# Selection moved, attention's background doubled, and the last output columns done block by block, in a one-core transformer block

## The chip, the cores and the metric

The kernel runs on one core of one Trainium2 chip. The metric is the device time of one execution in microseconds (us), as the median of several runs; lower is better. The engines are TensorE (PE in the profile; PEld is its weight load), VectorE (DVE), ScalarE (ACT), GpSimd (POOL) and SyncE (SP), whose queue issues most of the DMAs.

## The reference

One block of a streaming encoder on `x` of 512 tokens x 4096, float32:

```
h = rmsnorm(x);  z = h @ w_in      # 4096 x 9808: q, c, qi, kix, wix, gate_a, pool_in, gate_b
I[t,s] = sum_h wix[t,h] * relu(qi[t,h] . kix[s])       # indexer, 16 heads of 64
sel    = the 128 best s of each t with s//64 <= t//64
ya[h]  = softmax(q[h] . (c[sel] w_uk[h])) @ c[sel] w_uv[h]      # 16 heads of 128, latent c of 512
yb     = ((trailing mean over 2/4/8/16 tokens - token) @ w_pool[g]) * scale     # 4 groups of 512
y      = [ya * silu(gate_a), yb * silu(gate_b)] @ w_out;  out = x + rmsnorm(y)
```

## The kernel before

All matmuls keep float32 accuracy: `split` (L67) makes of each operand a high part (a ScalarE cast to fp32r) and a low part (a VectorE subtraction), and `mm3` (L80) does three matmuls of them. Tiles of 128 x 512 are the unit; `ts(b, P)` is block b of 128.

The stages, with their times in the profile before:

- *First projection* (to about 130 us): latent `c` and the indexer's key. `staged` (L71) loads 256 KB of weights into the pool `st` and splits them; `st` lies on the right side of SBUF, which is filled downwards from the top of the memory (`side="right"`); `big` tiles with tags p0 to p7 and d0 to d7 lie on the left.
- *Indexer queries* (to 300) with `dots` on the background queue, and four gate groups (to 373).
- *Products* (373 to 976): the first 16 k-blocks of the remaining 60 groups are multiplied with seven products instead of eight (`PRODUCTS`, L337), in 120 steps of 42 matmuls of 256 columns (loop L475). `s_weights` loads the weights two steps ahead; `form_weights` (L340) makes three differences on VectorE (L341 to L343) and splits into `wh` and `wl`, 2 casts and 2 subtractions. `collect_z` (L459) sums the products; GpSimd's queue stores them in `zpd`. The operands are `xp` (p slots) and `xs` (d slots: slot di is read in the steps with t = i//2). In the last pair the k-blocks 16 to 31 come back from `xsp` into the p slots, eight loads of 1 MB on GpSimd's queue (L491).
- *Pooling mixer, groups 0 to 2* (993 to about 1280). `group` (L299) loads the stored part of a group into a `zt` slot, `stream` (L270) adds the other 16 k-blocks (48 matmuls of 512 columns) with weights from `st`, and steps the background queue `bg` (L314) at three places of four and once after the end.
- *Attention* (first score at 1278, last at 1828): the loop L744 does two groups for each of 16 heads (query, gate); `attn` (L693) of a head is a generator on `bg`: two steps of keys, four of scores and softmax, for each fourth head four of values, four of transposes (L733) and products, two at the end. `bg.drain()` finishes what the groups left.
- *Pool group 3* (to 1945) with `st3` on the left side, and sums for the next stage copied into d slots (`sums_early`).
- *Output, first 20 k-blocks* (to about 2354) as seven products over `order`.
- *Output, last 12 k-blocks* (EB; to 2630): for each of 8 column blocks db, all 12 k-blocks e times the row blocks b. W (`wout[db, e]`) is loaded and split by `prefetch` into a ring of four (`rot_raw`, `rot_hi`, `rot_lo`). `lanes` (L806) gives db 0 to 5 all four row blocks at once; db 6 and 7 come twice, first for blocks 0 and 1, then for 2 and 3. After a lane VectorE adds the first part, ScalarE sums the squares, and `yg` keeps the product with the post gain. `finish` (L902) forms the row norm, does `yg * ry + x` and stores; for blocks 0 and 1 it runs on `bg` during the last lanes, for 2 and 3 behind the last matmul.

`select` (L510) repeats 16 times: the eight largest scores of a row (MAX8) and their replacement, for three row blocks; then it writes the mask `mb`. It is traced behind the products and added to `bg`. The framework fixes the order of each engine's instructions when the program is built: in the order of the trace, but a ready instruction may be put into an engine's modelled gap ahead of earlier ones that aren't ready. A tile's slot is given to the next tile when all its readers are done.

Of the kernel before, what the change touches and what calls it, by code (L numbers as in the profile page):

```python
# [36 lines left out]
NFULL = 6  # L37
# [4 lines left out]
NFS = 4  # L42
# [10 lines left out]
def block_kernel(ctx: ExitStack, tc: tile.TileContext, xT, x, gk, wc, wkw, wf, ws, wd, wuk, wuv, kvn,  # L53
# [4 lines left out]
    bigp = ctx.enter_context(tc.tile_pool(name="big", bufs=1))  # L58
    st_stack = ctx.enter_context(ExitStack())
# [279 lines left out]

    def form_weights(w, pool, bufs=1):  # L340
        V.tensor_sub(w[:, 4:6], w[:, 1:3], w[:, 0:2])  # L341
        V.tensor_sub(w[:, 6], w[:, 2], w[:, 4])
        V.tensor_sub(w[:, 7], w[:, 3], w[:, 6])  # L343
        hi = pool.tile([P, 7, H], F32R, tag="wh", name="wh", bufs=bufs)
        lo = pool.tile([P, 7, H], F32R, tag="wl", name="wl", bufs=bufs)
        split(w[:, 0:3:2], hi[:, 0:2], lo[:, 0:2])
        split(w[:, 3:8], hi[:, 2:7], lo[:, 2:7])
        return hi, lo
# [124 lines left out]

    with tc.tile_pool(name="pa", bufs=2, side="right", reuse_waits="tile") as pa:
        for n, (m, t) in enumerate(order_s):  # L475
# [24 lines left out]
            if n + 2 < len(order_s):  # L500
                first[n + 2] = s_weights(n + 2)
            bg.step()
        bg.drain()
    wa_stack.close()
    st_stack = ctx.enter_context(ExitStack())
    st = st_stack.enter_context(tc.tile_pool(name="st", bufs=4, side="right", reuse_waits="tile"))
    zt["tags"] = ("d6", "d7")
    mb = big("d5", [P, OFF[4]], "mb", F32)

    def select():  # L510
        V.memset(mb[:, :P], 0.0)
        V.memset(mb[:CHUNK, CHUNK:P], NEG)
        for b in range(1, NB):
            V.memset(isc[:CHUNK, OFF[b + 1] - P - CHUNK:OFF[b + 1] - P], INADM)
        yield
        for r in range(TOPK // 8):
            for b in range(1, NB):
                o = score(b)
                m8 = kixp.tile([P, 8], F32, name="m8", bufs=4)
                V.max(m8, o)  # L520
                V.match_replace(o, m8, o, TAKEN)
                if b != 2:
                    yield
        for b in range(1, NB):
            V.tensor_scalar(mb[:, OFF[b]:OFF[b + 1]], score(b), -3.2e38, NEG,
                            op0=ALU.is_gt, op1=ALU.mult)
            yield

    bg.add(select())
# [10 lines left out]

    ops = {}
# [37 lines left out]
    def pool_group(pl, pm, g):  # L579
# [77 lines left out]
        def rest():  # L657
            def early(q):
                if q == 2:
                    for e in sum_part(7, ow, "wr", 2, lambda sh, n: big("d6", sh, n)):  # L660
                        pass

            zt.update(n=0, tags=("d7",))
# [26 lines left out]
    with tc.tile_pool(name="at", bufs=1, reuse_waits="tile") as at:  # L690
# [53 lines left out]
        for h in range(NH):  # L744
# [8 lines left out]
            group(Q + h, evac)  # L753
            sg = at.tile([P, S], F32, tag="sg", name="sga", bufs=2)
            bg.add(attn(h, qp, sg))
            group(GA + h, lambda z, sg=sg: gate(at, z, sg))
# [6 lines left out]
    with tc.tile_pool(name="pl1", bufs=1, reuse_waits="tile") as pl:  # L763
# [4 lines left out]
        def sums_early():  # L768
# [4 lines left out]
            for t in range(6):  # L773
                for w in sum_part(t + 1, cw, "cw", 1, lambda sh, n: big(f"d{t}", sh, n)):
                    yield
# [30 lines left out]
    lanes = [(db, (0, 1, 2, 3)) for db in range(NFULL)]  # L806
    lanes += [(db, p) for p in ((0, 1), (2, 3)) for db in range(NFULL, 8)]
    steps = [(n, e) for n in range(len(lanes)) for e in range(EB)]
# [11 lines left out]
    def rot_split(src, hi=None, lo=None):  # L820
        raw = rotate("raw", "p0", F32)
        nc.sync.dma_start(raw, src)
        if hi is None:
            hi, lo = rotate("hi", "d0", F32R), rotate("lo", "p1", F32R)
# [3 lines left out]
    CT = ("d1", "p2", "d2", "p3", "d3", "p4")  # L828
    SPARE = ("d4", "p5", "d5", "p6", "d6", "p7", "d7")
# [9 lines left out]
    def prefetch(n):  # L839
        if n < len(steps) and n not in ahead:  # L840
            lane, e = steps[n]
            if n < EB:
                load_cat(e)
            ahead[n] = rot_split(wout[lanes[lane][0], e])

    for n, (db, i) in enumerate(order):
# [11 lines left out]
        if db == 0:  # L858
            if i == 0:
                pure_part(7, load_quads(7, oc, "pt", 1), lambda sh, m: big("p6", sh, m))  # L860
            if i == 1:
                late = sum_part(8, oc, "pt", 1, lambda sh, m: big("d7", sh, m))
# [22 lines left out]
    home, yg, xs, pp = {}, {}, {}, {}  # L885
# [7 lines left out]
    def fetch():  # L893
        for m, (b, db) in enumerate([(b, db) for p in ((0, 1), (2, 3)) for db in range(8) for b in p]):
            if m < 16:
                xs[b, db] = spare(2 * NFULL + m)
            else:
                xs[b, db] = opl.tile([P, 512], F32, name=f"xr{m}")
            nc.sync.dma_start(xs[b, db], x[b, db])
            yield  # L900
# [16 lines left out]
    for n, (lane, e) in enumerate(steps):  # L917
        db, blocks = lanes[lane]
        if e == 0:
            yp = [bank("acc" if i == 3 else "w") for i in range(len(blocks))]  # L920
            if lane == 1:
                bg.add(fetch())
            if lane == NFULL + 8 - NFULL:
                bg.add(finish((0, 1)))
        prefetch(n)
        wo = ahead.pop(n)
        for i, b in enumerate(blocks):
            mm3(yp[i], tuple(t[:, ts(b, P)] for t in ct[e]), wo, e == 0, e == EB - 1)
        if e == 3:
            pg = opl.tile([P, 512], F32, name="pg", bufs=2)  # L930
            nc.sync.dma_start(pg, gpost[:, ts(db, 512)].to_broadcast([P, 512]))
            for b in blocks:
                pp[b] = opl.tile([P, 512], F32, name="pp", bufs=6)
                nc.sync.dma_start(pp[b].rearrange("p (a c) -> p a c", a=2),
                                  part[db, :, b // 2::2, ts(b % 2, H)])
        if e == EB - 1:
            prefetch(n + 1)
            prefetch(n + 2)
            for i, b in enumerate(blocks):
                V.tensor_add(pp[b], yp[i], pp[b])  # L940
            for i, b in enumerate(blocks):
                junk = opl.tile([P, 512], mybir.dt.bfloat16, name="junk")
                A.activation(junk, pp[b], AF.Square, accum_out=yss[b][:, db:db + 1])
# [85 lines left out]
```

## Time and profile before

| what | value |
|---|---|
| median of 3 runs | 2641.9 us (2641.01 to 2643.49) |
| profiled execution, own time | 2648.14 us |
| its span | 2646.4 us |
| TensorE busy | 2554.5 us, 97% |
| VectorE busy | 1718.2 us, 65% |
| ScalarE busy | 1046.7 us, 40% |
| granted TensorE clock, mean | 0.984 |
| DMA | 377.39 MB, 143 GB/s |

Shares are averages over the stages. Matmuls are pipelined: their printed duration is longer than the distance to the next, so their rate is read from the starts or from a count in a stretch. Some matmul records can be missing.

### The profile page before, as it was taken

Reading aid. Unit: us, or ns where it says so; the run is one execution under the profiler, and the core shown is the slowest. Engines: PE = TensorE matmul, PEld = TensorE weight load, DVE = VectorE, ACT = ScalarE, POOL = GpSimd, SP = SyncE. Lnnn points to the kernel's source line nnn. Section 1 sums busy time; section 2 is a strip of 40 time slices with the busy share of each in tenths; the row PEclk is TensorE's granted clock in tenths of the full one; section 3 lists DMA queues with packets and bytes.
Section 4 is the critical chain, followed back from the end, with each engine's and each line's share of the span. In section 5 each row is a group of like instructions: output and inputs, shape, how many; then the busy total and the mean of one; then the engine's idle time right before and its main releaser. Section 6 shows DMA issues by size and latency. Waiting matters only on the chain. (4 is left out here: it accounts for less than half of the span.)

```text
span 2646.4 us, 39505 instructions
## 1 busy us (share of the span) xinstructions
PE 2554.5 (97%) x15322; PEld 2267.3 (86%) x15322; DVE 1718.2 (65%) x3034; ACT 1046.7 (40%) x1724; POOL 77.6 (3%) x138
## 2 busy tenths in 40 slices
PE   9999999999999979999999999987999999999996
PEld 7799889999999977888888888765789999998875
DVE  5465798878888765554445454555787877864347
ACT  6444524444444433222333333333344444443333
POOL 0000001000000010000000000000000000000000
PEclk9999999999999999999999999988999999999998
DMA  9733423433433463444333333312453433386457
GB/s 329 261 114 110 155 80 130 134 128 131 141 128 130 135 256 126 143 129 121 117 103 105 99 100 101 99 60 76 159 160 120 136 121 120 134 268 198 139 161 245
DMA packets 167260, 377.39 MB, mean 143 GB/s; under 512 B 19872, under 2 KB 28192, under 8 KB 165024
## 3 DMA queue, kind: packets, MB, share of 16 engines
q1 hardware_dynamic: 156736, 332.92, 39.1%
q0 software_dynamic: 10336, 41.95, 4.3%
q8 instruction: 120, 1.97, 0.3%
q14 instruction: 68, 0.56, 0.1%
HBM read 324.46 MB, written 50.33 MB: 142 GB/s over the span
## 5 line engine op out<-in xcount | busy, mean ns | idle before, releaser
L68 ACT CAST wh<-wr 128x512 fp32r<-128x512 f32 (+1 forms) x400 | 362.1, 943 | 488.0 <-PE ps_acc L488 265.6
L69 DVE TENSOR_TENSOR lo<-raw,hi 128x512 fp32r<-128x512 f32 x416 | 286.1, 689 | 396.3 <-ACT hi L68 396.0
L69 DVE TENSOR_TENSOR wl<-wr,wh 128x512 fp32r<-128x512 f32 (+1 forms) x400 | 434.9, 1088 | 122.4 <-ACT wh L68 120.3
L68 ACT CAST hi<-raw 128x512 fp32r<-128x512 f32 x416 | 257.1, 619 | 614.5 <-PE ps_acc L83 417.9
L82 PE MATMUL ps_acc<-xr,hi 128*128 128x512 f32 x928 | 373.6, 403 | 21.5 <-ACT hi L68 21.5
L83 PE MATMUL ps_acc<-xr,hi 128*128 128x512 f32 x928 | 368.6, 397 | 0.0
L84 PE MATMUL ps_acc<-xr,lo 128*128 128x512 f32 x928 | 368.1, 397 | 0.0
L82 PEld LDWEIGHTS ps_acc<-xr,hi 128*128 128x128 f32 x928 | 176.5, 190 | 60.2 <-ACT hi L68 21.9
L84 PEld LDWEIGHTS ps_acc<-xr,lo 128*128 128x128 f32 x928 | 175.8, 189 | 42.6 <-DVE lo L69 0.5
L83 PEld LDWEIGHTS ps_acc<-xr,hi 128*128 128x128 f32 x928 | 176.2, 190 | 38.5
L487 PE MATMUL ps_w<-xp,wl 128*128 128x256 f32 x720 | 203.8, 283 | 5.4 <-DVE wl L69 5.3
L486 PE MATMUL ps_w<-xp,wh 128*128 128x256 f32 x720 | 203.2, 282 | 0.0
L488 PE MATMUL ps_w<-xp,wh 128*128 128x256 f32 x720 | 203.2, 282 | 0.0
L488 PE MATMUL ps_w<-xs,wh 128*128 128x256 f32 x720 | 203.1, 282 | 0.0
L487 PE MATMUL ps_w<-xs,wl 128*128 128x256 f32 x720 | 202.9, 282 | 0.0
L486 PE MATMUL ps_w<-xs,wh 128*128 128x256 f32 x720 | 202.8, 282 | 0.0
L341 DVE TENSOR_TENSOR wr<-wr 128x512 f32<-128x512 f32 x200 | 137.7, 689 | 54.1 <-DMA wr<-in_ws 27.7
L69 DVE TENSOR_TENSOR rot_lo<-rot_raw,rot_hi 128x512 fp32r<-128x512 f32 x120 | 80.8, 689 | 139.6 <-ACT rot_hi L68 139.4
L487 PEld LDWEIGHTS ps_w<-xp,wl 128*128 128x128 f32 x720 | 136.2, 189 | 6.4 <-DVE wl L69 6.4
L854 PE MATMUL ps_w<-wl,op 128*128 128x256 f32 x480 | 136.9, 285 | 4.2 <-DVE wl L69 4.1
L68 ACT CAST rot_hi<-rot_raw 128x512 fp32r<-128x512 f32 x120 | 74.1, 621 | 168.5 <-PE ps_acc L84 112.8
L486 PEld LDWEIGHTS ps_w<-xp,wh 128*128 128x128 f32 x720 | 136.1, 189 | 0.0
(310 smaller groups left out, 6002.4 us busy)
## 6 DMA issues: line engine op xcount, KB each, us to landing
wr<-in_ws SPq DMA_DIRECT2D x120, 512.0 KB, 3.4
raw<-in_wd SPq DMA_DIRECT2D x240, 256.0 KB, 2.6
wr<-in_wq SPq DMA_DIRECT2D x80, 512.0 KB, 3.5
rot_raw<-in_wout SPq DMA_DIRECT2D x120, 256.0 KB, 3.4
raw<-in_wf SPq DMA_DIRECT2D x96, 256.0 KB, 2.6
zt<-zpd SPq DMA_DIRECT2D x60, 256.0 KB, 2.7
cw<-cat SPq DMA_DIRECT2D x34, 256.0 KB, 3.0
raw<-in_wc SPq DMA_DIRECT2D x32, 256.0 KB, 5.6
```

What stands on the lines that cost most here:

```text
L68: A.copy(hi, src)
L69: V.tensor_sub(lo, src, hi.bitcast(F32))
L82: nc.tensor.matmul(dst, lh, rh, start=start, stop=False)
L83: nc.tensor.matmul(dst, lh, rl, start=False, stop=False)
L84: nc.tensor.matmul(dst, ll, rh, start=False, stop=stop)
L341: V.tensor_sub(w[:, 4:6], w[:, 1:3], w[:, 0:2])
L486: nc.tensor.matmul(zz, w0, x0, start=i == 0 and j % 2 == 0, stop=False)
L487: nc.tensor.matmul(zz, w1, x0, start=False, stop=False)
L488: nc.tensor.matmul(zz, w0, x1, start=False, stop=last)
L854: nc.tensor.matmul(zz, ab[0], wl[:, w], start=False, stop=False)
```

## The change

1. A tile `edge` of 8 floats per partition (32 bytes) is put at the top of the right side, so all other tiles there lie 32 bytes lower.
2. `select` runs in the loop of the products: its first part at step 6, its instructions placed behind the first difference of the last `form_weights` (`issue_after`); one further part at each third step. `mb` lies in d2 instead of d5, and is written at the end of it.
3. `zt` uses d0 and d1 instead of d6 and d7; the later uses of the d slots are permuted (`DT`).
4. In attention the groups step the background twice at each place instead of once.
5. Output: db 0 to 6 do all four row blocks at once; for db 7 the split W of e = 4 to 11 is made during db 6 (`hold`) and kept with e = 0 to 3 of the ring, and the row blocks are done one after the other, each followed by its `leave` and `finish`. `x` for blocks 0 and 1 is fetched from db 1 on, for block b + 2 behind the finish of block b, into the same slots.

```diff
TAKEN = -3.4e38
-NFULL = 6
+NLAST = 7
 H = S // 2
...
 NA = 8
-NFS = 4
+LATE = 6
 OUT_SHAPE = (NB, 8, P, 512)
...
     bigp = ctx.enter_context(tc.tile_pool(name="big", bufs=1))
+    edge = ctx.enter_context(tc.tile_pool(name="edge", bufs=1, side="right"))
+    edge.tile([P, 8], F32, name="edge")
     st_stack = ctx.enter_context(ExitStack())
...
+    mark = {}
     def form_weights(w, pool, bufs=1):
-        V.tensor_sub(w[:, 4:6], w[:, 1:3], w[:, 0:2])
+        mark[0] = V.tensor_sub(w[:, 4:6], w[:, 1:3], w[:, 0:2]).ins
         V.tensor_sub(w[:, 6], w[:, 2], w[:, 4])
...
+    masks = []
+    def select():
+        for b in range(1, NB):
+            V.memset(isc[:CHUNK, OFF[b + 1] - P - CHUNK:OFF[b + 1] - P], INADM)
+        yield
+        for r in range(TOPK // 8):
+            for b in range(1, NB):
+                o = score(b)
+                m8 = kixp.tile([P, 8], F32, name="m8", bufs=4)
+                V.max(m8, o)
+                V.match_replace(o, m8, o, TAKEN)
+                if b != 2:
+                    yield
+        mb = big("d2", [P, OFF[4]], "mb", F32)
+        masks.append(mb)
+        V.memset(mb[:, :P], 0.0)
+        V.memset(mb[:CHUNK, CHUNK:P], NEG)
+        for b in range(1, NB):
+            V.tensor_scalar(mb[:, OFF[b]:OFF[b + 1]], score(b), -3.2e38, NEG,
+                            op0=ALU.is_gt, op1=ALU.mult)
+            yield
+    picks = select()
     with tc.tile_pool(name="pa", bufs=2, side="right", reuse_waits="tile") as pa:
...
                 first[n + 2] = s_weights(n + 2)
+            if n == LATE:
+                with tc.issue_after(mark[0]):
+                    next(picks)
+            elif n > LATE and n % 3 == 0 and n < len(order_s) - 4:
+                next(picks, None)
             bg.step()
         bg.drain()
+    for _ in picks:
+        pass
+    mb = masks[0]
     wa_stack.close()
...
     st = st_stack.enter_context(tc.tile_pool(name="st", bufs=4, side="right", reuse_waits="tile"))
-    zt["tags"] = ("d6", "d7")
-    mb = big("d5", [P, OFF[4]], "mb", F32)
...
-    bg.add(select())
+    zt["tags"] = ("d0", "d1")
...
+    DT = [f"d{i}" for i in (3, 4, 5, 6, 7, 2, 0, 1)]
     ops = {}
...
                 if q == 2:
-                    for e in sum_part(7, ow, "wr", 2, lambda sh, n: big("d6", sh, n)):
+                    for e in sum_part(7, ow, "wr", 2, lambda sh, n: big(DT[6], sh, n)):
                         pass
-            zt.update(n=0, tags=("d7",))
+            zt.update(n=0, tags=("d1",))
             group(GB - ONCE + 4 * g + 1, evs[1], before=None, after=early)
...
-            group(Q + h, evac)
+            group(Q + h, evac, 2)
             sg = at.tile([P, S], F32, tag="sg", name="sga", bufs=2)
             bg.add(attn(h, qp, sg))
-            group(GA + h, lambda z, sg=sg: gate(at, z, sg))
+            group(GA + h, lambda z, sg=sg: gate(at, z, sg), 2)
         bg.drain()
...
             for t in range(6):
-                for w in sum_part(t + 1, cw, "cw", 1, lambda sh, n: big(f"d{t}", sh, n)):
+                for w in sum_part(t + 1, cw, "cw", 1, lambda sh, n: big(DT[t], sh, n)):
                     yield
...
-    lanes = [(db, (0, 1, 2, 3)) for db in range(NFULL)]
-    lanes += [(db, p) for p in ((0, 1), (2, 3)) for db in range(NFULL, 8)]
-    steps = [(n, e) for n in range(len(lanes)) for e in range(EB)]
+    steps = [(db, e) for db in range(NLAST + 1) for e in range(EB)]
     ahead, ct, late = {}, {}, []
...
         if hi is None:
-            hi, lo = rotate("hi", "d0", F32R), rotate("lo", "p1", F32R)
+            hi, lo = rotate("hi", DT[0], F32R), rotate("lo", "p1", F32R)
         split(raw, hi, lo)
...
-    CT = ("d1", "p2", "d2", "p3", "d3", "p4")
-    SPARE = ("d4", "p5", "d5", "p6", "d6", "p7", "d7")
+    CT = (DT[1], "p2", DT[2], "p3", DT[3], "p4")
+    SPARE = (DT[4], "p5", DT[5], "p6", DT[6], "p7", DT[7])
     cts = {}
...
         if n < len(steps) and n not in ahead:
-            lane, e = steps[n]
+            db, e = steps[n]
             if n < EB:
                 load_cat(e)
-            ahead[n] = rot_split(wout[lanes[lane][0], e])
+            ahead[n] = rot_split(wout[db, e])
...
             if i == 1:
-                late = sum_part(8, oc, "pt", 1, lambda sh, m: big("d7", sh, m))
+                late = sum_part(8, oc, "pt", 1, lambda sh, m: big(DT[7], sh, m))
                 next(late)
...
     yss = [opl.tile([P, 8], F32, name=f"yss{b}") for b in range(NB)]
-    home, yg, xs, pp = {}, {}, {}, {}
+    home, yg, xs, pp, kept = {}, {}, {}, {}, {}
...
-    def fetch():
-        for m, (b, db) in enumerate([(b, db) for p in ((0, 1), (2, 3)) for db in range(8) for b in p]):
-            if m < 16:
-                xs[b, db] = spare(2 * NFULL + m)
-            else:
-                xs[b, db] = opl.tile([P, 512], F32, name=f"xr{m}")
-            nc.sync.dma_start(xs[b, db], x[b, db])
-            yield
+    def fetch(blocks):
+        for b in blocks:
+            for db in range(8):
+                xs[b, db] = spare(8 * (b % 2) + db)
+                nc.sync.dma_start(xs[b, db], x[b, db])
+                yield
+    def hold(e):
+        n = 2 * (e - 4)
+        pair = []
+        for i in (n, n + 1):
+            t, j = divmod(i, 4)
+            if t == 3:
+                pair.append(opl.tile([P, S], F32R, name=f"wx{j}"))
+                continue
+            if t not in kept:
+                kept[t] = big(SPARE[4 + t], [P, 4, S], f"kept{t}")
+            pair.append(kept[t][:, j])
+        ahead[NLAST * EB + e] = rot_split(wout[NLAST, e], *pair)
...
-    for n, (lane, e) in enumerate(steps):
-        db, blocks = lanes[lane]
+    def partials(db):
+        pg = opl.tile([P, 512], F32, name="pg", bufs=2)
+        nc.sync.dma_start(pg, gpost[:, ts(db, 512)].to_broadcast([P, 512]))
+        for b in range(NB):
+            pp[b] = opl.tile([P, 512], F32, name="pp", bufs=6)
+            nc.sync.dma_start(pp[b].rearrange("p (a c) -> p a c", a=2),
+                              part[db, :, b // 2::2, ts(b % 2, H)])
+        return pg
+    def leave(db, blocks):
+        for b in blocks:
+            V.tensor_add(pp[b], yp[b], pp[b])
+        for b in blocks:
+            junk = opl.tile([P, 512], mybir.dt.bfloat16, name="junk")
+            A.activation(junk, pp[b], AF.Square, accum_out=yss[b][:, db:db + 1])
+            yg[b, db] = opl.tile([P, 512], F32, tag="ya", name="yg", bufs=32)
+            V.tensor_mul(yg[b, db], pp[b], pg)
+    def product(db, e, b):
+        mm3(yp[b], tuple(t[:, ts(b, P)] for t in ct[e]), ahead[db * EB + e], e == 0, e == EB - 1)
+    for n, (db, e) in enumerate(steps):
+        if db == NLAST:
+            break
         if e == 0:
-            yp = [bank("acc" if i == 3 else "w") for i in range(len(blocks))]
-            if lane == 1:
-                bg.add(fetch())
-            if lane == NFULL + 8 - NFULL:
-                bg.add(finish((0, 1)))
+            yp = [bank("acc" if b == 3 else "w") for b in range(NB)]
+            if db == 1:
+                bg.add(fetch((0, 1)))
         prefetch(n)
-        wo = ahead.pop(n)
-        for i, b in enumerate(blocks):
-            mm3(yp[i], tuple(t[:, ts(b, P)] for t in ct[e]), wo, e == 0, e == EB - 1)
+        for b in range(NB):
+            product(db, e, b)
+        del ahead[n]
         if e == 3:
-            pg = opl.tile([P, 512], F32, name="pg", bufs=2)
-            nc.sync.dma_start(pg, gpost[:, ts(db, 512)].to_broadcast([P, 512]))
-            for b in blocks:
-                pp[b] = opl.tile([P, 512], F32, name="pp", bufs=6)
-                nc.sync.dma_start(pp[b].rearrange("p (a c) -> p a c", a=2),
-                                  part[db, :, b // 2::2, ts(b % 2, H)])
+            pg = partials(db)
+        if db == NLAST - 1 and e < EB - 4:
+            hold(e + 4)
         if e == EB - 1:
...
             prefetch(n + 2)
-            for i, b in enumerate(blocks):
-                V.tensor_add(pp[b], yp[i], pp[b])
-            for i, b in enumerate(blocks):
-                junk = opl.tile([P, 512], mybir.dt.bfloat16, name="junk")
-                A.activation(junk, pp[b], AF.Square, accum_out=yss[b][:, db:db + 1])
-                if b >= 2 and db < NFULL:
-                    yg[b, db] = spare(2 * db + b - 2)
-                else:
-                    yg[b, db] = opl.tile([P, 512], F32, tag="ya", name="yg", bufs=16)
-                V.tensor_mul(yg[b, db], pp[b], pg)
+            leave(db, range(NB))
         else:
...
     bg.drain()
-    for _ in finish((2, 3)):
-        pass
+    prefetch(NLAST * EB + 2)
+    prefetch(NLAST * EB + 3)
+    pg = partials(NLAST)
+    yp = [bank("acc" if b == 3 else "w") for b in range(NB)]
+    for b in range(NB):
+        for e in range(EB):
+            product(NLAST, e, b)
+        leave(NLAST, (b,))
+        for _ in finish((b,)):
+            pass
+        if b < 2:
+            for _ in fetch((b + 2,)):
+                pass
```

## Rows read from the trace of the kernel before

**Rows 1.** The page, part 1: busy time, share of the span, instructions.
```profile
PE 2554.5 (97%) x15322; PEld 2267.3 (86%) x15322; DVE 1718.2 (65%) x3034; ACT 1046.7 (40%) x1724; POOL 77.6 (3%) x138
```

**Rows 2.** Stretches: length, busy us of PE, PEld, DVE, ACT, POOL; clock, DMA share, GB/s.
```profile
330.00:377.00 47.00, 43.66 (x208) 35.92 (x206) 47.00 (x132) 12.94 (x19) 2.17 (x4) 1.00 0.22 72
373.00:387.00 14.00, 9.61 (x58) 9.41 (x57) 12.01 (x27) 2.40 (x3) 0.00 (x0) 0.76 0.23 75
600.00:900.00 300.00, 299.65 (x2524) 299.44 (x2523) 246.23 (x391) 136.35 (x180) 26.68 (x45) 1.00 0.40 132
976.00:999.00 23.00, 5.96 (x18) 4.59 (x17) 5.00 (x9) 3.77 (x7) 2.34 (x4) 0.63 0.94 353
1050.00:1250.00 200.00, 200.00 (x855) 160.80 (x854) 109.60 (x187) 56.60 (x92) 0.00 (x0) 1.00 0.44 134
1300.00:1700.00 400.00, 400.00 (x1817) 325.74 (x1816) 188.90 (x380) 134.75 (x263) 0.00 (x0) 1.00 0.34 102
1709.00:1842.00 133.00, 99.32 (x411) 71.99 (x409) 78.36 (x209) 51.21 (x124) 0.00 (x0) 0.84 0.19 59
2354.00:2630.00 276.00, 268.05 (x1172) 218.82 (x1170) 130.80 (x215) 96.61 (x188) 1.62 (x3) 0.99 0.60 194
2380.00:2555.00 175.00, 175.00 (x774) 144.91 (x773) 71.16 (x111) 55.67 (x112) 0.00 (x0) 1.00 0.51 160
```

**Rows 3.** Timeline of ScalarE before 380: start, us, what.
```profile
369.08 1.78 ACT L68 CAST wh<-wr 128x512 fp32r<-128x512 f32 x2
```

**Rows 4.** Timeline of VectorE in the same stretch.
```profile
368.82 1.15 DVE L520 MAX8 m<-isc 128x8 f32<-128x384 f32 x2
...
374.74 1.15 DVE L520 MAX8 m<-isc 128x8 f32<-128x384 f32 x2
...
377.32 0.68 DVE L69 TENSOR_TENSOR wl<-wr,wh 128x512 fp32r<-128x512 f32 x1
```

**Rows 5.** Timeline of TensorE there: idle time before and its releaser in brackets.
```profile
378.05 0.58 PE L487 MATMUL ps_w<-xp,wl 128*128 128x256 f32 x1 [4.39 <-DVE wl L69]
```

**Rows 6.** Groups of ScalarE instructions in 600 to 900: busy, mean ns, idle.
```profile
L68 ACT CAST wh<-wr 128x512 fp32r<-128x512 f32 x120 | 107.5, 944 | 139.1 <-PE ps_acc L488 137.6 <-DVE wr L343 1.5
```

**Rows 7.** Groups of VectorE instructions in 600 to 900.
```profile
L69 DVE TENSOR_TENSOR wl<-wr,wh 128x1280 fp32r<-128x1280 f32 x121 | 132.2, 1092 | 40.1 <-ACT wh L68 39.4
```

**Rows 8.** Waits in 960 to 1000: total us, times, longest.
```profile
PE ps_acc L82 <- ACT hi L68: 17.0, 1, 17.0
ACT hi L68 <- DMA raw<-in_wd: 15.8, 1, 15.8
```

**Rows 9.** DMA issues in 950 to 1003: count, KB each, us to landing.
```profile
xr<-xsp POOLq DMA_DIRECT2D x8, 1024.0 KB, 8.2
...
zt<-zpd SPq DMA_DIRECT2D x5, 256.0 KB, 12.9
```

**Rows 10.** Line 733, the transposes of probabilities, in two stretches (PE, PEld only).
```profile
1270.00:1709.00 439.00, 16.81 (x90) 11.92 (x90) 1.00 0.34 102
1709.00:1842.00 133.00, 20.27 (x70) 12.69 (x70) 0.84 0.19 59
```

**Rows 11.** Waits in 1709 to 1842.
```profile
ACT pth L68 <- PE ps_w L733: 19.5, 13, 1.7
...
PE ps_w L733 <- DVE prob L714: 16.3, 18, 1.9
```

**Rows 12.** Timeline of VectorE at the end of the span.
```profile
2628.38 1.37 DVE L940 TENSOR_TENSOR pp<-ps_w,pp 128x512 f32<-128x512 f32 x2 [3.06 <-PE ps_w L84]
...
2632.45 8.04 DVE L913 SCALAR_TENSOR_TENSOR xr<-sp,ry,xr 128x512 f32<-128x512 f32 x12
```

**Rows 13.** Timeline of TensorE, the mixer's products of the last pool group.
```profile
1892.46 0.39 PE L82 MATMUL ps_w<-mh,hi 128*128 128x512 f32 x1
...
1893.14 0.39 PE L82 MATMUL ps_w<-mh,hi 128*128 128x512 f32 x1
...
1894.55 0.39 PE L82 MATMUL ps_acc<-xr,hi 128*128 128x512 f32 x1
```

More of the change, by code (lines that the diff above doesn't have):

```diff
@@ L506, in block_kernel @@
     st = st_stack.enter_context(tc.tile_pool(name="st", bufs=4, side="right", reuse_waits="tile"))
-    zt["tags"] = ("d6", "d7")
-    mb = big("d5", [P, OFF[4]], "mb", F32)
[L510 to L514, printed above, removed]
-        yield
[L516 to L527, printed above, removed]
-    bg.add(select())
+    zt["tags"] = ("d0", "d1")
     def gate(pool, z, sg):
@@ L891, in spare @@
         return home[t][:, j]
-    def fetch():
-        for m, (b, db) in enumerate([(b, db) for p in ((0, 1), (2, 3)) for db in range(8) for b in p]):
-            if m < 16:
-                xs[b, db] = spare(2 * NFULL + m)
-            else:
-                xs[b, db] = opl.tile([P, 512], F32, name=f"xr{m}")
-            nc.sync.dma_start(xs[b, db], x[b, db])
-            yield
+    def fetch(blocks):
[16 more added lines that the diff above has]
+        ahead[NLAST * EB + e] = rot_split(wout[NLAST, e], *pair)
     def finish(blocks):
```

## Prediction

> **What bounds the kernel now.** I read the page first: TensorE is busy for nearly the whole span [rows 1], so a gain can come from two places only: stretches in which TensorE waits or runs at its lower clock, and matmuls that take longer than they need. Then I cut the span into stretches [rows 2]. In most TensorE is busy from end to end at a granted clock of 1.00 (600 to 900, 1050 to 1250, 1300 to 1700, 2380 to 2555): there only the pitch of a matmul counts. Four stretches lose time: 373 to 387, 976 to 999, 1709 to 1842, and the output stage from 2354. Last I read, for each of these, the timeline or the waits, to see whose lateness it is.
>
> **Selection, its old place.** In 330 to 377 VectorE is busy for all 47 us [rows 2]: the selection's pieces run back to back. ScalarE's cast of the first weight tile `wh` was issued at 369.08, but VectorE came to its low part `wl` at 377.32 only [rows 3, 4], and TensorE waited 4.39 us for it [rows 5] and then ran at a granted clock of 0.76 (a mixture of 2.4 and 1.2 GHz). Stretch 373 to 387 holds 58 matmuls; the product stage's pitch is 300 us / 2524 = 0.119 us [rows 2], so they need 6.9 us and the stretch loses 7.1. With selection started only behind the `form_weights` of step 8 this queue is gone: -7.1. Behind `wl` stood nothing else of TensorE's.
>
> **Selection, its new place.** Two of its rounds take 374.74 - 368.82 = 5.92 us [rows 4]; 16 rounds take 47.4 us of VectorE. The product stage has 113 steps left, of 42 matmuls, 4.99 us each; VectorE is busy 246 of 300 us there [rows 2], which leaves 0.9 us a step, 101 us in all. So it fits: load 82% becomes 91%. The cover is thin, though. A step's chain is two casts (0.94 us each on average [rows 6]) and the second `wl` (at least 1.09, and 2.18 if both stand in line [rows 7]): 3.0 to 4.1 of 4.99 us, a slack of 0.9 to 2.0. One selection piece (1.15/2 = 0.57 us [rows 4]) in front of `wl` is absorbed; two or three aren't. The order on each engine is set when the program is built, and in the kernel before ready work of later parts was put into VectorE's gaps so densely that `wl` came some 7 us late. Lower bound 0 (all in gaps), upper bound half of the 47.4 us, +24. I take +5, nearer to the row of the product stage itself, in which TensorE loses 0.35 of 300 us. The moved memsets are few and small; the three mask writes still come at the stage's end.
>
> **Slots and the gap at 976.** The last product ends near 976; TensorE then waits 17.0 us for the first group's weights, and ScalarE, which casts them, 15.8 us for their load [rows 8]; TensorE restarts at the lower clock. 976 to 999 holds 18 matmuls, some 4 us of work: 19 us lost. Two things hold that load back: SP issues it behind the loads of `zt`, which need slots d6 and d7, read by the last products; and the eight 1 MB loads of `xr` fill the DMA engines (busy share 0.94, 353 GB/s [rows 2]; a load of `zt` took 12.9 us to land [rows 9]). With `zt` in d0 and d1, freed about 15 us earlier, SP is past that wait sooner, but the bytes stay the same. Bounds 0 and -8; I take -4.
>
> **Attention.** A chance to step the background comes three times in a group and once after it: 8 in a head's two groups. A head's attention needs 12 steps, 16 for each fourth head, 13 on average. So the 16 heads' groups (128 chances) carry fewer than 10 heads, and the trace shows it: transposes of probabilities, 10 a head, number 90 up to 1709 and 70 after it [rows 10]. Seven heads run behind the last group with nothing beside them, in 133 us. Their own work, by the code's columns: scores, keys, outputs and transposes 15,104 columns a head, values 24,576 each fourth head, 21,248 on average; at the 0.234 us for 512 columns of 1050 to 1250 that is 9.7 us a head, 68 for seven. 65 us are lost, to waits for `prob` (16.3) and behind the ScalarE and VectorE copies of `pth` and `ptl` (19.5 and the like) and to a clock of 0.84 [rows 2, 11]. With two steps a chance, 16 are offered for each head: all are done beside the groups but the last head's 3 or 4, which with the change of pools I leave at 7 us. -58. For cover: in 1300 to 1700 TensorE is busy 400 of 400 us and VectorE 189; 16 heads in the place of 9 bring VectorE to some 60%. Bounds: -63 (nothing left) and -40 (a quarter or so of the waits remains).
>
> **Output columns.** The 12 blocks' products are 1,152 matmuls. In 2380 to 2555 they run at 175/774 = 0.226 us; 2354 to 2630 holds 1,172, or 265 us of its 276 [rows 2]. About 10 us are lost (the last matmul is over soon after 2628.4, where the last sums begin [rows 12]), most of them in db 6 and 7, where W is loaded and split twice and `finish` of the first two blocks stands among the splits on VectorE. 24 loads and splits go (0.69 us of VectorE each), the held W of db 7 is formed during db 6, where VectorE is 41% busy. I leave 2 us at the two changes of stage: -8. **Tail**: behind the last products VectorE does 2 adds (1.37), multiplies, and 16 final operations at 8.04/12 = 0.67 us [rows 12]; the span (2646.4) ends 18.0 us after the adds began. With one block left an add, a multiply and 8 final operations go: 0.7 + 0.6 + 5.4 = 6.7. A block's products last 36 x 0.226 = 8.1 us, its `leave` and `finish` on VectorE about as long (8 x 0.67 + 1.3 + 1.5 = 8.2), so it may be a little late: -6.5. Loads of `x` for blocks 2 and 3 wait on the SP queue for the stores of blocks 0 and 1, and land a block ahead. Together -14.5, bounds -18 and -8. The permuted d slots I cost at 0: the copies into them run under the last pool groups, which keep TensorE busy.
>
> **Alignment.** The 32-byte `edge` moves every tile of the right side from 96 to 64 bytes past a multiple of 128 (by the sizes of the tiles above them). It matters if operands' addresses do: 512-column matmuls with `hi` and `lo` from the right side run at 200/855 = 0.234 us, those of the output, with all on the left, at 0.226 [rows 2]: 7.8 ns apart. 3,792 matmuls touch `st` on the right side (384 first projection, 384 gates, 960 + 144 pool, 1,536 + 384 attention): a full cure is worth -29. Against it: in the last pool group, whose weights lie on the left, three matmuls with `mh`, `ml` of the first channel tile take 0.68 us, the next six, whose operands lie at 64 past 128, 1.41, so 0.235 each [rows 13]. That is the nearest row, and by it 64 is hardly better than 96. But those are moving operands, `hi` and `lo` are mostly stationary. I take -4 and keep 0 and -29.
>
> The Trainium skill ("SBUF — State Buffer", "Specifications (TRN2)") gives SBUF lines of 16 bytes; by that rule a shift of 32 bytes changes no operand's place in a line, and the term would be 0 and the forecast 2563. The trace agrees no further than that something of the address or side does change the pitch, 0.234 against 0.226 us.
>
> **Sum.** -7.1 + 5 - 4 - 58 - 14.5 - 4 = -82.6. The profiled execution took 2648.1 us, 6.2 over the median of the runs; I take the difference over: 2565.5 for a profiled one, 2641.9 - 82.6 = 2559.3 for the median.
>
> **Rivals.**
> - *The alignment cures all*: -29 for -4: 2534. For it: 7.8 ns on thousands of matmuls; against it rows 13. 0.27.
> - *The edge does nothing*: 2563, 0.06 (the rule above).
> - *Selection makes the product stage VectorE's*: +22 in place of +5: 2576. For it: rows 3 and 4; against it the 18% of slack. 0.16.
> - *Attention's gain is half*, because the chains of two steps in one chance aren't filled by matmuls of the group: -27: 2590. For it: 0.9 us for each wait on `prob`; against it the full 400 us with one step. 0.10.
> - *The other side: not faster.* The same mechanism at full price: TensorE, in order, stands still in every chance between the first step's transposes and the second step's products. There are 128 chances; the change loses all when a chance costs 82.6/128 = 0.65 us beyond what is now expected, and at the 0.9 us of rows 11 it would be 128 x 0.9 = 115 us: 2674. Against it: group matmuls whose weights are there are put between. 0.03.
> - *The gap at 976 stays or grows*, since more of the DMA queue collides: 2568. 0.04.
>
> **The numbers.** The forecast itself holds 0.34, its own range 2545 to 2572. The rest as above. 0.2% (5 us) is about what a measurement of this kernel can tell from no change: faster 0.96, same 0.01, slower 0.03. For 8 in 10 the range takes in the full cure (2534, less some 10 for the other terms' good ends) and half of attention's gain (2590): 2524 to 2594. What lies outside are sums of several good ends (down to 2517) or bad ones.
>
> **What would show it.** No wait for `wl` near 378; MAX8 spread from some 410 on, and TensorE's waits for `wl` between 410 and 700 below 5 us in all; a gap of some 13 us at the end of the products; transposes of the 16th head within some 10 us of the last attention group and no stretch at 0.84; 96 of `rot_lo` in the place of 120; some 11.5 us from the last matmul to the end; pitch in the pool stage 0.233 (full cure: 0.227). Wrong would be: VectorE at 100% with repeated waits for `wl` and a lower clock among the products; waits for `prob` and `pth` all along attention; a pitch in the pool stage that has gone to 0.227, or risen.

## The result and the profile after

The changed kernel takes 2584.1 us in the median of four runs (2578.7 to 2586.5), the kernel before 2641.7: a ratio of 0.978 (95% interval 0.976 to 0.980), 58 us less. The forecast was 2559 with a range of 2524 to 2594: the sign and the large term were right, the gain was forecast 25 us too large. The profiled execution took 2584.8 us with a span of 2583.0, 63.4 less than the span before (whose execution stood 6 us above its median).

The same stretches as in [rows 2], of the kernel after, with the same columns:

```profile
330.00:377.00 47.00, 47.00 (x241) 39.50 (x241) 12.18 (x17) 12.02 (x18) 2.17 (x4) 1.00 0.22 73
373.00:387.00 14.00, 14.00 (x121) 14.00 (x120) 9.64 (x13) 6.17 (x8) 0.00 (x0) 1.00 0.30 107
600.00:900.00 300.00, 300.00 (x2530) 299.95 (x2529) 246.60 (x392) 137.14 (x181) 26.91 (x47) 1.00 0.38 133
976.00:999.00 23.00, 8.55 (x24) 6.33 (x25) 4.75 (x9) 3.09 (x5) 1.79 (x3) 0.63 0.78 290
1050.00:1250.00 200.00, 200.00 (x860) 161.30 (x859) 108.66 (x186) 56.19 (x91) 0.00 (x0) 1.00 0.43 134
1300.00:1700.00 400.00, 400.00 (x1864) 324.56 (x1863) 219.41 (x471) 149.85 (x315) 0.00 (x0) 1.00 0.33 104
```

The reader is to see: near 378 TensorE no longer waits (121 matmuls in 14 us, 58 before); the gap behind the products is still there, with 24 matmuls in the 23 us that held 18 before; the pool stage holds 860 matmuls in 200 us in place of 855, a pitch of 0.2326 against 0.2339.

The waits of TensorE in the kernel after between 373 and 1010 (total us, times, longest), then those in 1250 to 1860, then the line of the selection (duration in ns, first and last start):

```profile
PE ps_acc L84 <- ACT hi L70: 12.6, 1, 12.6
PE ps_w L515 <- DVE wl L71: 4.4, 10, 1.1
PE ps_acc L86 <- DVE lo L71: 2.6, 1, 2.6
```

```profile
PE ps_acc L84 <- ACT hi L70: 6.6, 1, 6.6
PE ps_w L85 <- DVE ptl L71: 0.9, 3, 0.3
PE ps_w L84 <- ACT pth L70: 0.7, 1, 0.7
```

```profile
L488 DVE MAX8 m<-isc x48: 361/548/691, 402.6 to 585.5; 128x8 f32<-128x256 f32 x16, 128x8 f32<-128x384 f32 x16, 128x8 f32<-128x512 f32 x16
```

One wait of 4.39 us for `wl` [rows 5], with two short ones later, has become ten of at most 1.1; seven of them lie between 469 and 598, where the selection now runs (403 to 586) or has just ended. In attention TensorE's waits for `prob` [rows 11] are gone; what is left is one wait of 6.6 us for the first weights of the next pool, and 1.6 us for `ptl` and `pth`. Of the 160 transposes of probabilities (columns as in [rows 10]) 130 now stand in the stretch that had 90, and the last is at 1779 in place of 1833:

```profile
1270.00:1709.00 439.00, 20.48 (x130) 16.47 (x130) 1.00 0.33 104
1709.00:1790.00 81.00, 4.57 (x30) 3.74 (x30) 0.97 0.26 81
```

The end of the span: the last matmul on TensorE, and VectorE's additions for row blocks 0 to 3 with the last block's final operations.

```profile
2562.97 0.40 PE L86 MATMUL ps_acc<-wx,ct 128*128 128x512 f32 x1
```

```profile
2541.04 0.69 DVE L953 TENSOR_TENSOR pp<-ps_w,pp 128x512 f32<-128x512 f32 x1 [6.43 <-PE ps_w L86]
...
2550.37 0.68 DVE L953 TENSOR_TENSOR pp<-ps_w,pp 128x512 f32<-128x512 f32 x1
...
2558.80 0.68 DVE L953 TENSOR_TENSOR pp<-ps_w,pp 128x512 f32<-128x512 f32 x1
...
2567.21 0.68 DVE L953 TENSOR_TENSOR pp<-ps_acc,pp 128x512 f32<-128x512 f32 x1
...
2570.32 5.39 DVE L938 SCALAR_TENSOR_TENSOR sp<-yg,ry,sp 128x512 f32<-128x512 f32 x8
```

The last matmul is over at about 2563.2 (2562.97 and a pitch of 0.23), but VectorE adds the last block's sum at 2567.2, 4.0 us late: it spends 9.3 us on the first block and 8.4 on each other one (2558.80 to 2567.21), TensorE 8.2, and it began late, at 2541.0. Its last operation is over at 2575.7, and the span ends 7.3 us later, with DMA engines full (12.6 MB between 2545 and the end). So the tail takes 20 us where the kernel before took 18.

### The profile page after: what moved, and what is told of

Its sections match the earlier page's. It is cut to its first block, busy times and chain, and to the rows that moved or that the text cites. A ratio compares the mean times of both kernels' runs of the same rounds, so it can differ in the third digit from the quotient of the medians.

```text
span 2583.0 us, 39314 instructions
## 1 busy us (share of the span) xinstructions
PE 2522.2 (98%) x15322; PEld 2248.5 (87%) x15322; DVE 1703.9 (66%) x3010; ACT 1033.4 (40%) x1700; POOL 77.3 (3%) x138
## 4 chain that ended last, share of the span: by engine, by line
issue 53%; PE 32%; DVE 9%; DMA 4%; ACT 1%; POOL 1%; SPq 0%; DVEq 0%; POOLq 0%; ACTq 0%
PE ps_w L515 4%; PE ps_w L516 4%; PE ps_w L514 4%; PE ps_w L85 3%; PE ps_w L84 3%; PE ps_w L86 3%; DVE wl L71 3%; PE ps_acc L84 3%; PE ps_acc L86 3%; PE ps_acc L85 3%; DMA wr<-in_ws 1%; DVE wr L345 1%; DMA xn<-in_x 1%; DVE isc L489 1%; DVE m L488 1%
## 5 line engine op out<-in xcount | busy, mean ns | idle before, releaser
L71 DVE TENSOR_TENSOR rot_lo<-rot_raw,rot_hi 128x512 fp32r<-128x512 f32 x88 | 60.0, 690 | 133.1 <-ACT rot_hi L70 133.1
L515 PEld LDWEIGHTS ps_w<-xs,wl 128*128 128x128 f32 x720 | 135.6, 188 | 0.0
```

The lines of the kernel that those rows point to most:

```text
L71: V.tensor_sub(lo, src, hi.bitcast(F32))
L515: nc.tensor.matmul(zz, w1, x0, start=False, stop=False)
```

## The experiments

Each kernel was timed beside the kernel before on the same chip; ratios are to it, with a 95% interval.

**Two steps in attention alone.**

```diff
-            group(Q + h, evac)
+            group(Q + h, evac, 2)
-            group(GA + h, lambda z, sg=sg: gate(at, z, sg))
+            group(GA + h, lambda z, sg=sg: gate(at, z, sg), 2)
```

> The kernel before, with two background steps at each chance in attention and nothing else changed. By the forecast's term: 58 us less than before, 2584. By a recount of the matmuls in 1709 to 1842 (it also holds 49 matmuls of groups and the values of one and a half heads, so fewer than 65 us are lost there): 46 us less, 2596, with 18 us of it or more at the clock's lower level gone, and first to last score 549.5 us before, some 503 here. If the other edits carry the gain: within 15 us of before, and waits for prob in place of the drain.

2598.0 against 2646.9: 0.981 (0.979 to 0.982), 51 us less (47 to 55). The forecast's 58 lies outside, the recount's 46.5 at the edge. In the trace, 130 transposes stand before 1709 and the waits of TensorE in 1250 to 1860 are those of the whole change:

```profile
PE ps_acc L82 <- ACT hi L68: 6.7, 1, 6.7
PE ps_w L83 <- DVE ptl L69: 0.9, 3, 0.3
PE ps_w L82 <- ACT pth L68: 0.7, 1, 0.7
```

The recount's rows are of the kernel before, the groups of TensorE instructions in 1709 to 1842:

```profile
L82 PE MATMUL ps_w<-cTh,hi 128*128 128x512 f32 x25 | 11.7, 468 | 0.0
L83 PE MATMUL ps_w<-cTl,hi 128*128 128x512 f32 x25 | 10.6, 424 | 0.0
L84 PE MATMUL ps_w<-cTh,lo 128*128 128x512 f32 x26 | 10.4, 399 | 0.0
L82 PE MATMUL ps_acc<-xr,hi 128*128 128x512 f32 x17 | 7.7, 456 | 4.5 <-ACT hi L68 4.5
L83 PE MATMUL ps_acc<-xr,hi 128*128 128x512 f32 x16 | 6.8, 425 | 0.0
L84 PE MATMUL ps_acc<-xr,lo 128*128 128x512 f32 x16 | 6.6, 413 | 0.0
```

49 matmuls of groups (17 + 16 + 16) were in the stretch that I had taken for heads alone, 49 x 0.234 = 11.5 us of work that no change removes; 58 - 11.5 = 46.5. The 51 measured lie between the two, and what makes up the other 4 us is not shown.

**The edge alone, three sizes, and on the changed kernel.**

```diff
     bigp = ctx.enter_context(tc.tile_pool(name="big", bufs=1))
+    edge = ctx.enter_context(tc.tile_pool(name="edge", bufs=1, side="right"))
+    edge.tile([P, 8], F32, name="edge")       # 16 in e10, 24 in e9 and e4
```

> The kernel before, with the 32-byte tile on the right side and nothing else changed. If addresses count a little: pitch of 512-column matmuls with the right side's weights 0.2344 to 0.2333 us, 4 us in all on 3,792 of them, and another 4 in the output's first 20 blocks, whose 256-column matmuls read their weights from there (411 us before): 4 to 8 us less. If only lines of 16 bytes count: no change, within 3 us. If 64 past 128 cures all: 29 us less, pitch 0.227.

> The kernel before, with a right-side tile of 64 bytes: right-side tiles at 32 past a multiple of 128. If the remainder by 64 counts: like the kernel before (96 past 128), pitch 0.234, no change. If the distance to the next multiple of 128 counts: between 32 and 96 bytes of edge, some 15 us less. If any shift does some good: 6 us, like 32 bytes.

> The kernel before, with a right-side tile of 96 bytes and nothing else changed: right-side tiles at a multiple of 128. If the address modulo 128 sets the pitch of 512-column matmuls: 0.234 to 0.227 us in the first projection, the pool groups and attention, 3,792 x 7 ns = 27 us, less what the 256-column matmuls of the products lose when they fall into their slower rhythm (0.119 to 0.120 us, up to 6 us): 20 to 27 us less than before. If the gain needed the other edits: 6 us, as with 32 bytes.

> The changed kernel with an edge of 96 bytes in place of 32, so that right-side tiles lie at 32 past a multiple of 128 in place of 64 if the distance from the top counts downwards, or at a multiple of 128 if the sizes were reckoned with the other sign. If a multiple of 128 cures the pitch and this is one: pitch 0.227 in the pool stage, 20 to 29 us less than the changed kernel, 2558. If only small phases count: within 6 us of it, pitch between 0.232 and 0.235. If only lines of 16 bytes count: no change.

| kernel | right-side tiles past a multiple of 128 | ratio to before |
|---|---|---|
| before, edge 32 bytes | 64 | 0.998 (0.997 to 0.999) |
| before, edge 64 bytes | 32 | 0.998 (0.997 to 0.999) |
| before, edge 96 bytes | 0 | 0.993 (0.991 to 0.994) |
| changed kernel, edge 96 bytes | 0 | 0.971 (0.969 to 0.972) |

The stretch 1050 to 1250 (pool stage) of e2, e10, e9 and e4, one fence each, columns as in [rows 2]:

```profile
1050.00:1250.00 200.00, 200.00 (x860) 161.30 (x859) 109.61 (x187) 57.01 (x92) 0.00 (x0) 1.00 0.44 134
```

```profile
1050.00:1250.00 200.00, 200.00 (x859) 161.04 (x859) 114.46 (x200) 57.99 (x94) 0.00 (x0) 1.00 0.44 135
```

```profile
1050.00:1250.00 200.00, 200.00 (x883) 165.35 (x882) 111.12 (x190) 56.37 (x93) 0.00 (x0) 1.00 0.45 139
```

```profile
600.00:900.00 300.00, 300.00 (x2503) 300.00 (x2502) 244.59 (x390) 136.66 (x180) 26.04 (x45) 1.00 0.40 131
...
1050.00:1250.00 200.00, 200.00 (x882) 165.29 (x881) 112.60 (x192) 57.83 (x95) 0.00 (x0) 1.00 0.45 138
```

The count is the reading: 855 before, 860 and 859 at 64 and 32 past 128, 883 and 882 at a multiple of 128, so 0.234, 0.233 and 0.2266 us. Only the last is the output's pitch. No other edit than the edge was made, so the shift does it, and with it the address. The remainders by 128 are my reckoning: no trace shows an address, and the expectation of e4 still left open whether 96 bytes lead to a multiple of 128. 32 bytes are worth 6 us (4 to 9), 96 are worth 20 (16 to 23) on the kernel before and 19 more on the changed one (0.9705 / 0.9778 = 0.9925, of 2584). Of the three expectations for 64 bytes the last held, that any shift does some good (5 us, 3 to 8); that the remainder by 64 or the distance to the next multiple decides was wrong. With 96 bytes, the 28 us that the counts promise didn't come whole. In the kernel before, probably, this is because the heads behind the last group wait for other engines and gain nothing from a faster matmul: in e9 TensorE's wait for `prob` in 1250 to 1860 is as long as before (16.3).

```profile
PE ps_w L735 <- DVE prob L716: 16.5, 18, 1.9
```

In the changed kernel the products run through 600 to 900 in a slower rhythm, 2,503 matmuls in place of 2,530, and the output's first 20 blocks take 411 us in place of 408.

**The output stage alone** (part 5 of the change on the kernel before, slots by their old names).

> The kernel before, with the new output stage of the last 12 blocks alone (slots as before). By the forecast: 14.5 us less, of which 6.5 behind the last matmul. By the trace of the change: 7 us less; matmuls end 9 us sooner, but the time from the last matmul to the end is 19 to 20 us in place of 17.5, because VectorE begins the last block's sum some 4 us late and the stores share full DMA engines with loads of x. If that lateness came from another edit: 18 us become 12.

2640.4 against 2646.9: 0.997 (0.996 to 0.999), 7 us less (4 to 11), as the trace of the change said and half of the forecast. Its matmuls end 9 us sooner, counted from the first to the last of the stage, and its tail is 19.4 us.

**Selection alone, and slots alone.**

```diff
 # e5: select() as in the change, but
...
+        mb = big("d5", [P, OFF[4]], "mb", F32)
...
 # e6
-    zt["tags"] = ("d6", "d7")
-    mb = big("d5", [P, OFF[4]], "mb", F32)
+    zt["tags"] = ("d0", "d1")
+    mb = big("d2", [P, OFF[4]], "mb", F32)
...
+    DT = [f"d{i}" for i in (3, 4, 5, 6, 7, 2, 0, 1)]     # and the later uses through DT
```

> The kernel before, with selection alone moved into the products' loop (mask still in d5, slots as before). By the forecast: the 7.1 us near 378 saved, 5 us lost to late wl among the products, 2 us less in sum. By the trace of the change: the stall at 378 is gone, and some 7 stalls of 0.3 to 0.6 us come between 460 and 600, with 2 to 3 us at the stage's end; products' stage 606 to 608 us, so 0 to 2 us less, within noise. If VectorE bounds the products in the other order: 10 us or more above the kernel before.

> The kernel before, with the slots alone: loads of the stored parts in d0 and d1, mask in d2, later d slots permuted. By the forecast: 4 us less, from the gap behind the products. By the trace of the change: first wait 17.3 to some 13 us, but a second of 3 us behind the first weights, and the lower clock until the same time, so 1.5 to 4 us less. If the eight 1 MB loads alone set the time of the first weights: first wait stays at 17 us, no change.

Selection: 2648.7 against 2650.0, 1.000 (0.999 to 1.001). Slots: 2651.8 against 2650.0, 1.001 (1.000 to 1.002). Neither can be told from nothing. TensorE's waits in 373 to 975 with selection moved, and in 370 to 1010 with the slots moved:

```profile
PE ps_w L514 <- DVE wl L70: 3.5, 8, 0.9
```

```profile
PE ps_acc L82 <- ACT hi L68: 13.8, 1, 13.8
PE ps_w L487 <- DVE wl L69: 6.6, 6, 3.0
PE ps_acc L84 <- DVE lo L69: 2.0, 1, 2.0
```

Selection pays its stall of 4.4 us back in eight small ones: in one profile, 373 to 387 holds 120 matmuls in e5 and 58 before, but 373 to 976 only 17 more (5,018 and 5,001), so 45 x 0.119 = 5.4 us of the gain were lost again. The slots do shorten the wait behind the products, 17.0 to 13.8 us, but a second one of 2.0 comes behind it, and the waits for `wl` grow from 5.3 to 6.6: two new ones stand in the last steps, and ScalarE waits for the last weights of the products (waits in 960 to 1000):

```profile
ACT wh L68 <- DMA wr<-in_ws: 6.0, 1, 6.0
```

The loads of `zt` start at 960.0 here, beside the last load of these weights (961.4), and at 973.9 in the kernel before; the slowest load of `wr` between 930 and 1000 takes 8.8 us to land, and 5.6 before. Whether the order of the queue or the full DMA engines delay it, no run tells apart.

**The tail: without x for blocks 2 and 3.**

```diff
-            for _ in fetch((b + 2,)):
-                pass
+            for d in range(8):
+                xs[b + 2, d] = xs[b, d]
```

> The changed kernel, leaving out the loads of x for row blocks 2 and 3 (the final operation adds what blocks 0 and 1 left in the slots). If full DMA engines delay the end: the last store lands some 3.3 us behind the last final operation in place of 7, 4 us less; VectorE still begins the last block's sum 4 us after its last matmul. If VectorE's lateness itself comes from late x: it begins with the last matmul, 8 us less. If neither: no change.

0.975 (0.974 to 0.977) to the kernel before, where the changed kernel has 0.978 (0.976 to 0.980): the direction is the expected one, but the intervals meet, so the size is read from one profile of each. In its trace VectorE is as late as in the changed kernel, but the span of 2579.4 ends 3.5 us behind its last operation in place of 7.3:

```profile
2567.46 0.68 DVE L953 TENSOR_TENSOR pp<-ps_acc,pp 128x512 f32<-128x512 f32 x1
...
2570.57 5.39 DVE L938 SCALAR_TENSOR_TENSOR sp<-yg,ry,sp 128x512 f32<-128x512 f32 x8
```

So two things lengthen the tail: 3.8 us are stores beside loads of `x`, 4.0 us are VectorE's lateness.

**A better version, and two of its parts.**

```diff
-    edge.tile([P, 8], F32, name="edge")
+    edge.tile([P, 24], F32, name="edge")
...
+        low = right.enter_context(tc.tile_pool(name="low", bufs=1, side="right", reuse_waits="tile"))
+        low.tile([P, 16], F32, name="low")
         ow = right.enter_context(tc.tile_pool(name="ow", bufs=1, side="right", reuse_waits="tile"))
...
-        for e in range(EB):
-            product(NLAST, e, b)
+        for e in (4, 5, 6, 7, 8, 9, 10, 11, 0, 1, 2, 3):
+            product(NLAST, e, b, 4, 3)          # start and stop flags follow
...
-            for _ in fetch((b + 2,)):           # gone in e8 and e11, kept in e12
-                pass
+        if b == 0:
+            free = big("p0", [P, 4, 512], "free", F32)     # loads of x[2, 0..3] into it
+        for d in range(4 if b == 0 else 0, 8 if b < 2 else 0):
+            xs[b + 2, d] = yg[b, d]             # and the load of x[b + 2, d]
...
+                with tc.issue_after(mark[0]):   # e11 only
                     next(picks, None)
```

> The changed kernel with an edge of 96 bytes, the output's first-stage weights 64 bytes lower again, in the last column block the held W first, and x of block 2 loaded into the free ring and into the finished block's own tiles as soon as these are free. From the edge 17 us less than the changed kernel (2588 to 2571 on the last chip); from the weights of the first 20 blocks, 256-column pitch 0.1200 to 0.1178 on 3,360 matmuls, some 4 to 7; from the tail 2 (first block's sums no longer wait for the last splits) and up to 4 from loads in DMA's idle time: 2558 to 2566. If the pitch doesn't follow the address but the moment: no gain from the 64 bytes; if VectorE alone sets the tail: 2 us there.

> The kernel of the run e8_best, with x of blocks 2 and 3 fetched as in the changed kernel (into the stored slots of blocks 0 and 1). If the early loads of x matter: 3 to 4 us above e8_best, the last stores landing 7 us behind the last final operation again. If the order of the held W alone made the tail's gain: the same as e8_best within 1 us.

> The kernel of the run e8_best, with each part of selection held behind the form_weights of its own step, so that it can't be put into earlier gaps. If the dense packing of selection between 460 and 600 makes the late wl: the 8 stalls of 0.3 to 0.7 us there go, MAX8 spreads over 400 to 950, 4 us less than e8_best. If any selection piece in front of wl stalls: as many stalls, spread out, no gain. If a piece held back delays the next form_weights: more and longer stalls, slower.

e8: 2561.9 against 2650.0, 0.967 (0.965 to 0.968), the fastest here: 3.3% below the kernel before, where the change gives 2.2%. e12: 0.967 (0.966 to 0.969); e11: 0.968 (0.967 to 0.969). The medians of the three can't be told apart. The output's first 20 blocks take 404 to 407 us in them, 411 in e4, which has the 96 bytes without the tile `low`. VectorE's first and last sum in the trace of e8, and its last matmul:

```profile
2518.78 0.69 DVE L955 TENSOR_TENSOR pp<-ps_w,pp 128x512 f32<-128x512 f32 x1 [4.18 <-PE ps_w L86]
...
2544.97 0.68 DVE L955 TENSOR_TENSOR pp<-ps_acc,pp 128x512 f32<-128x512 f32 x1
```

```profile
2542.97 0.39 PE L86 MATMUL ps_acc<-rot_hi,ct 128*128 128x512 f32 x1
```

VectorE adds the last sum 1.8 us behind the last matmul in place of 4.0, and the tail is 16.0 us; in e12, with the same lateness, it is 17.7. So the order of the held W gives 2.2 us, and the early loads of `x` 1.7, in one profile each, where 3 to 4 were expected for them. From VectorE's first sum to the end of the last matmul are 24.4 us in e8, three blocks of TensorE's 8.2; in the changed kernel they are 22.2. There TensorE had done some ten matmuls of later blocks before it finished block 0. Pacing the selection spread MAX8 from 415 to 887, yet TensorE's waits for `wl` in 373 to 975 are 5.6 us in 8, where e8 has 4.7 in 11:

```profile
PE ps_w L515 <- DVE wl L71: 5.6, 8, 1.1
```

So fewer and longer waits, and no gain: that the dense packing makes them is not borne out.

## Why the forecast was right in its sign and too large

*Selection.* -7.1 and +5 were both close. In 373 to 387 stand 121 - 58 = 63 more matmuls, 63 x 0.119 = 7.5 us; the waits for `wl` cost 4.4 us in all, and with selection alone 5.4 us are lost behind that point by the count of matmuls. Alone selection measured 0 (-3 to +2); -2 was forecast, and the run can't tell the two apart.

*Slots.* -4 failed: alone the slots measured +2 (-1 to +4.5). The step that failed is the one that took the wait for what follows from the load's start alone: behind `zt` loads that start earlier, where the DMA engines are full (busy share 0.94 in [rows 2]), the last weights of the products came later and a second wait stood behind the first weights; that the one takes from the other is argued from these two waits. I had written that the bytes stay the same, and still took half of the bound.

*Attention.* The mechanism was right: all heads beside the groups, no stretch at 0.84 left (0.97), 6.6 us at the change of pools for the 7 allowed. The term was mis-sized, 51 measured for 58: the 65 us lost came from columns that I counted by the code for seven heads "with nothing beside them", where the stretch held 49 matmuls of groups too (by that recount 46.5). The 19.5 us of [rows 11] that I named among the losses are ScalarE's waits for TensorE; TensorE itself stood still for 34 of the 133 us, and its clock was 0.84 [rows 2]. A list of the instructions in the stretch would have shown it.

*Output.* The products gained 9 us for 8. The tail was forecast at -6.5 and came at +2: VectorE 4.0 us late, stores 3.8 us late. The prediction had the first in hand (8.2 us a block against 8.1) and let it pass as "a little late". It missed that the first block's sum would be ready only at 2541.0: its last W come from splits that stand behind `leave` of the column block before, and TensorE's order puts matmuls of later blocks ahead of them; e8, which takes the held W first, more than halves the lateness. It also missed that VectorE needs 9.3 us for the first block, 1.2 of them waiting for ScalarE's square root. The second it had checked only for whether `x` lands in time, not for whether stores land late behind those loads.

*Alignment.* -4 for the matmuls of 512 columns was close (the pool stage's 1.3 ns on 3,792 are 5 us; the edge alone measured 6), and the nearest row [rows 13] was the right guide for 64 past 128. The rival of a full cure named the right pitch and the wrong shift: 96 bytes give 0.2266, and measured 20 us for its 29. The remainders were put down "by the sizes of the tiles above them", but `st` is the first pool on the right side and nothing stands above it; they fit the runs and are not shown by them. By the rule of the Trainium skill ("SBUF — State Buffer", "Specifications (TRN2)"), 16-byte lines, neither 32 nor 96 bytes would move an operand's place in a line; the trace doesn't agree that the shift is worth nothing: 855, 860 and 883 matmuls in 200 us. The term left out the 256-column matmuls of the output's first 20 blocks, 411 to 407 us in e2 from the first to the last.

*Sum.* The parts alone give -51 - 7 - 6 - 0.5 + 2 = -63, the whole gave -58 (-54 to -63): they add up within what was measured. Of the 25 us that were forecast and didn't come, 7 are attention's, 9 the tail's, 5 to 6 the slots'; the rest is within the intervals. Of the rivals, only the last came in part: the gap behind the products stayed in its effect.

## What to carry to other kernels

Before a stretch is called empty, list what ran in it: one query of the instructions by group would have taken 11 us out of the largest term. When work is reordered so that one stage finishes piece by piece, reckon each engine's time for a piece against the others' and the DMA bytes of the last pieces against what the engines move; a piece that is level by 0.1 us can't make up for a late start. And where matmuls of one shape show two pitches, try the address of their operands: a tile of 96 bytes, which does nothing else, was worth 20 us.

## What the runs showed of the hardware

The pitch of 512-column matmuls follows the shift of the operand on the right side: in the pool stage 0.234 us in the kernel before, 0.233 with 32 and 64 bytes, 0.2266 with 96; by my reckoning these lie 96, 64, 32 and 0 past a multiple of 128. There the operand is the stationary one. In the first projection it is the moving one, and the mean distance of neighbouring starts goes from 0.233 us to 0.228 with 96 bytes (e9). The 384-column matmuls of the indexer queries, whose stationary operand lies there too, keep 0.173 to 0.174 us at every shift. Matmuls of 256 columns behave otherwise again: the output's first 20 blocks, whose moving operand lies on the right, took 411 us with 96 bytes (e9), as in the kernel before; with 32 they took 407 (e2), 408 (the changed kernel) and 405 (the run without x), and 409 with 64 (e10). And they have more than one rhythm at the same addresses. In the run without x the stretches 1960 to 2040 and 2100 to 2180 of that stage hold 695 and 669 matmuls with nearly the same busy time:

```profile
1960.00:2040.00 80.00, 79.38 (x695) 79.18 (x694) 63.44 (x92) 34.97 (x41) 1.62 (x3) 1.00 0.39 131
2100.00:2180.00 80.00, 78.94 (x669) 78.59 (x668) 63.04 (x90) 32.57 (x41) 2.69 (x5) 1.00 0.39 127
```

The products show it too (from 2,530 down to 2,503 in e4 and 2,499 in e10 in 600 to 900, with their operands on the left side in all). What sets the rhythm stays open; it is worth up to 4 us in 300.
